# Low weight parts of a float32 hybrid decoder: a negated copy and an adding DMA in place of a subtraction

## The chip, the cores and the metric

One core of a Trainium2 chip runs the kernel. The metric is the device time of one execution in microseconds (us). The core has a matrix engine (TensorE, PE in the rows; its weight loads stand as PEld), VectorE (DVE), ScalarE (ACT), GpSimd (POOL), a queue engine that here only issues transfers (SyncE, SP), and 16 DMA engines that all queues share. Each engine works through its own instructions in a fixed order and waits on semaphores for the others.

## The reference, cut to what matters

Two layers, on 512 tokens of 1024 features, everything in float32. Each layer has one input projection with 78 column tiles of 128, three token mixers (SSD, S5 and latent attention, MLA), and an output projection:

```
for l in range(DEPTH):                       # DEPTH = 2
    h = rms_norm(x, pre_norm[l])
    proj = h @ w_in[l]
    z_a, xbc, dt_raw, u_b, z_b, c_q, c_kv, k_rope, z_c, gate_logits = split_columns(proj)
    y_a = ssd_branch(z_a, xbc, dt_raw, ...) @ w_a[l]
    y_b = s5_branch(u_b, z_b, ..., w_glu[l], b_glu[l]) @ w_b[l]
    y_c = mla_branch(c_q, c_kv, k_rope, z_c, ...) @ w_c[l]
    merged = gates[0] * y_a + gates[1] * y_b + gates[2] * y_c
    x = x + rms_norm(merged @ w_o[l], post_norm[l])
```

## The kernel before, in words

A product of two float32 matrices is made out of three products of rounded numbers. Each operand is split into a high part, rounded to the format `F32R` that TensorE multiplies in one pass, and a low part, the float32 operand minus its high part; the kernel adds high times high, high times low and low times high in PSUM. Weights come from DRAM in blocks of 128 partitions by up to 1024 columns, 512 KiB, and each is used once, for 512 tokens.

`weight` (L85) does this for one block. SyncE loads it into a buffer `wf` (L95, or eight pieces at L93 for one operand of S5), ScalarE writes the rounded copy `wh` (the call at L96, whose instruction carries the helper's line L59), and VectorE writes `wl = wf - wh` (the call at L98, instruction line L71). In the MLA stage every third block and in the SSD stage every second has its subtraction on GpSimd instead (L74; `lo_pool` and the counter `nw` choose). `wf`, `wh` and `wl` have two buffers each, so `wf` of one block is free for the load of the block after the next as soon as the subtraction has read it. `dense` (L101) then runs, per block of 1024 columns, 16 matmuls that read `wh` (L109, L110) and after them 8 that read `wl` (L112), all 128x128 by 512 columns. `mm3` (L52) is the other user: it goes through high-high, high-low and low-high for each 128 rows, so it needs `wl` almost at once (L54 to L56); the first two tiles of each layer (`proj2`), the key and value tiles of MLA and the S5 blocks take that way.

A layer runs in this order: norm and the first projection tiles; MLA, with the preparation of the S5 matrices woven in (mostly multiplications on GpSimd); a scan over 63 steps that lies on VectorE, beside the `w_c` products; SSD; eight S5 blocks, each with two blocks of S5 matrices (`kpad` in pieces, `odr`) that go through `weight` from a pool of their own; then the `w_glu`, gate and `w_b` products, and the output projection. Six of the eight output blocks `w_o` are loaded between the `w_b` products (L1043, L1044): they take a `wf` buffer out of the same two, but are split by `split` (L76) into buffers of their own. The order of the instructions on each engine comes from a scheduler that simulates the program when it is built; it is no part of the source.

Of the kernel before, what the change touches and what calls it, by code (L numbers as in the profile page):

```python
# [17 lines left out]
L = 2  # L18
# [5 lines left out]
# first tile of each part of the input projection, in the host's order  # L24
# [10 lines left out]
class Trunk:  # L35
# [49 lines left out]
    def weight(self, src, n, pool=None):  # L85
        """hi and lo parts of a block of n columns per partition, streamed from DRAM"""
        pool = pool or self.wp
        wf = pool.tile([P, 1024], F32, name="wf", tag="wf", bufs=2)
        wh = pool.tile([P, 1024], F32R, name="wh", tag="wh", bufs=2)
        wl = pool.tile([P, 1024], F32R, name="wl", tag="wl", bufs=2)  # L90
        if isinstance(src, list):
            for rows, x in src:
                self.nc.sync.dma_start(wf[rows, :n].rearrange("p (g k) -> p g k", k=x.shape[-1]), x)  # L93
        else:
            self.nc.sync.dma_start(wf[:, :n], src)  # L95
        self.act_(wh[:, :n], wf[:, :n])  # L96
        self.nw += 1
        (self.gt if self.lo_pool and self.nw % self.lo_pool == 0 else self.tt)(wl[:, :n], wf[:, :n], wh[:, :n].bitcast(F32), ALU.subtract)  # L98
        return wh, wl

    def dense(self, src, rhs, m=P, n=None, main=True):  # L101
        """[m, T] bank of src^T rhs; rhs: (hi, lo) per 128 rows"""
        k = len(rhs)
        wh, wl = self.weight(src, k * m)
        ps = self.bank(main)
        mm = self.nc.tensor.matmul
        o = lambda i: slice(i * m, i * m + m)
        for i, (bh, bl) in enumerate(rhs):
            mm(ps[:m], wh[:, o(i)], bh, start=i == 0, stop=False)  # L109
            mm(ps[:m], wh[:, o(i)], bl, start=False, stop=False)  # L110
        for i, (bh, bl) in enumerate(rhs):
            mm(ps[:m], wl[:, o(i)], bh, start=False, stop=i == k - 1)  # L112
        return ps

    def proj2(self, l, tiles):
        """two tiles of the projection, first for the first half of the tokens"""
# [57 lines left out]
    def sincos_small(self, ang, n):  # L174
# [21 lines left out]
        # sin = 2 s c, cos = 1 - 2 s^2  # L196
# [8 lines left out]
    def rsqrt_mean(self, ss, n, scale, eps=EPS):  # L205
        """(scale * ss + eps) ** -0.5 on n columns"""
# [6 lines left out]
    def rsqrt_rows(self, sq, scale):  # L213
        """sq [128, T]: sums over partitions -> (scale * sum + eps) ** -0.5 along T, on every partition"""
# [13 lines left out]
    def s5_prep(self, l, pp):  # L228
# [27 lines left out]
        # f = (abar - 1) / lambda  # L256
# [18 lines left out]
        # coefficients of the scan over blocks: groups 0..31 on the lower half, 32..63 on the upper  # L275
# [25 lines left out]
        def block(b):  # L301
            """inputs in blocks of 8 steps: (step, channel of the group) on partitions; what depends on B and C alone"""
# [49 lines left out]
        def back(b, s, uf, bb, v1, w1):  # L352
# [19 lines left out]
            if s % 2:  # L372
# [3 lines left out]
                # kernel of the steps within a block  # L376
# [32 lines left out]
    def norm_in(self, tt, xt, G):  # L409
        """RMS norm of a tile of tokens (two halves of its features), transposed and split into self.hh, self.hl"""  # L410
# [15 lines left out]
    def silu2(self, l, tile_, keep=True):  # L426
        """2 silu of a tile of the projection"""
# [24 lines left out]
    def merge(self, l, i, w, acts, m, rrow=None):  # L452
        """merged += 2 sigmoid(gate_i) * (w^T acts) (* rrow along T), a tile of it; its gates run ahead"""
# [137 lines left out]
    def attend_qk(self, mp, q, k, h):  # L591
        """rows of exp(q k^T * SCALE - max), causal; their sums in self.rs"""
# [19 lines left out]
    def attend_v(self, mp, scs, v):  # L612
        """probabilities times v, transposed, as the sum of two parts of [64, T]"""
        nc = self.nc
        # key block kb holds queries kb * 128 ...
# [25 lines left out]
    def ssd_dt(self, l, sp):  # L641
        """dt, its cumulative decays and what depends on tokens and heads alone"""
# [55 lines left out]
    def ssd(self, l):  # L698
        nc, tc, a = self.nc, self.tc, self.a
        with tc.tile_pool(name=f"ssd{l}", bufs=1, reuse_waits="tile") as sp:  # L700
# [12 lines left out]
            def conv(t):  # L713
                """silu of the causal convolution of a tile of channels"""
# [16 lines left out]
            def core(g, xs, zs, bt, ct):  # L731
# [4 lines left out]
                # C B^T per chunk, keys on partitions, masked  # L736
# [7 lines left out]
                # token-major x dt, its decayed form, and B  # L744
# [26 lines left out]
                # states at the chunks' starts  # L771
# [50 lines left out]
            def head(g, hh, cbm):  # L822
                """decayed C B^T of a head, keys on partitions, and its decays along T"""
# [46 lines left out]
    def s5_scan(self, l, sp):  # L870
        """states at the starts of the blocks"""
# [14 lines left out]
    def s5_block(self, l, sp, b):  # L886
        """outputs of 8 groups, and their gelu"""
# [66 lines left out]
    def layer_in(self, l, xs):  # L954
        """xs(t): the two halves of x of a tile of 128 tokens, in SBUF"""
# [7 lines left out]
    def layer(self, l):  # L963
        nc, tc, a = self.nc, self.tc, self.a
        self.first2 = self.proj2(l, (CQ, CQ + 1))
        # rope key and dt
# [17 lines left out]
    def mix(self, l):  # L984
        nc, tc, a = self.nc, self.tc, self.a
        with ExitStack() as st:
# [6 lines left out]
            # the softmax's sums, along T  # L993
# [73 lines left out]
    def wout(self, l, mg, wo, G):  # L1067
        nc = self.nc

        def out_tile(t):  # L1070
# [18 lines left out]
            # the rows are twice the reference's: 0.5 (s / 4 + eps) ** -0.5 = (s + 4 eps) ** -0.5  # L1089
# [52 lines left out]
def _tiles(w):  # L1142
    """[L, K, M] -> [L, M / 128, 128 (row), K / 128, 128 (column)]"""
    l, k, m = w.shape
    w = w.reshape(l, k // P, P, m // P, P).transpose(0, 3, 2, 1, 4)
    return np.ascontiguousarray(w).reshape(l, m // P, P, k)


def layouts(i):
# [31 lines left out]
    # constants  # L1181
# [32 lines left out]
```

## Time and profile before

| | us |
|---|---|
| median of 2 runs | 2004.49 (2004.17 to 2004.82) |
| span of the profiled execution | 2005.7 |
| PE busy | 1890.3 |
| DVE busy | 1451.9 |
| ACT busy | 942.0 |
| POOL busy | 649.9 |

The span goes from the first to the last instruction of one profiled execution. Busy time of matmuls counts each from its start to its modelled end, though the next one starts earlier, so a PE that is nearly always busy can still have room. In the rows, an arrow points from what an instruction reads to what it writes (`wl<-wf,wh`); a bracket gives the idle time before an instruction and what ended it.

### The profile page before, as it was taken

Reading aid. Unit: us, or ns where it says so; the run is one execution under the profiler, and the core shown is the slowest. Engines: PE = TensorE matmul, PEld = TensorE weight load, DVE = VectorE, ACT = ScalarE, POOL = GpSimd, SP = SyncE. Lnnn points to the kernel's source line nnn. Section 1 sums busy time; section 2 is a strip of 40 time slices with the busy share of each in tenths; the row PEclk is TensorE's granted clock in tenths of the full one; section 3 lists DMA queues with packets and bytes.
Section 4 is the critical chain, followed back from the end, with each engine's and each line's share of the span. In section 5 each row is a group of like instructions: output and inputs, shape, how many; then the busy total and the mean of one; then the engine's idle time right before and its main releaser. Section 6 shows DMA issues by size and latency. Waiting matters only on the chain.

```text
span 2005.7 us, 27806 instructions
## 1 busy us (share of the span) xinstructions
PE 1890.3 (94%) x9688; PEld 1524.2 (76%) x9688; DVE 1451.9 (72%) x2845; ACT 942.0 (47%) x1743; POOL 649.9 (32%) x743
## 2 busy tenths in 40 slices
PE   7897999899999989999997999998999999999998
PEld 6685777687877868887875777776878887788786
DVE  7866667699999857744478666677999996776433
ACT  4364566522555445533333655564235563554331
POOL 1855466301333201201118556662013331012010
PEclk9898999899999999999998999998999999999999
DMA  5232234232321266344232333342332224662531
GB/s 166 88 115 83 91 118 128 83 108 74 127 74 64 75 184 181 93 152 157 88 91 83 108 104 111 91 139 82 96 123 77 74 74 111 181 171 84 168 126 42
DMA packets 132605, 219.96 MB, mean 110 GB/s; under 512 B 36208, under 2 KB 75760, under 8 KB 131952
## 3 DMA queue, kind: packets, MB, share of 16 engines
q1 hardware_dynamic: 132464, 218.19, 35.4%
q8 instruction: 76, 1.25, 0.3%
q14 instruction: 65, 0.53, 0.1%
HBM read 182.08 MB, written 31.33 MB: 106 GB/s over the span
## 4 chain that ended last, share of the span: by engine, by line
PE 59%; DVE 25%; DMA 7%; POOL 3%; ACT 3%; issue 2%; SPq 1%; DVEq 0%; POOLq 0%; ACTq 0%
PE mm L109 14%; PE mm L110 13%; PE mm L112 13%; DVE wl L71 4%; DVE keep L62 3%; PE mm L54 2%; PE mm L55 2%; PE mm L56 2%; DMA wf<-in_w_in 2%; DVE ms L882 2%; DVE sc_t L879 2%; PE pk L378 2%; DVE ms L881 1%; PE aux L55 1%; PE aux L54 1%
## 5 line engine op out<-in xcount | busy, mean ns | idle before, releaser
L109 PE MATMUL mm<-hh,wh 128*128 128x512 f32 (+1 forms) x1232 | 501.2, 407 | 16.4 <-DVE ql L71 8.8
L110 PE MATMUL mm<-hl,wh 128*128 128x512 f32 (+1 forms) x1232 | 493.6, 401 | 0.0
L59 ACT ACTIVATE wh<-wf 128x1024 fp32r<-128x1024 f32 (+1 forms) x294 | 291.2, 994 | 423.7 <-PE mm L110 240.8
L71 DVE TENSOR_TENSOR wl<-wf,wh 128x1024 fp32r<-128x1024 f32 (+1 forms) x243 | 297.5, 1229 | 183.8 <-ACT wh L59 149.6
L112 PE MATMUL mm<-hh,wl 128*128 128x512 f32 (+1 forms) x1232 | 315.1, 393 | 2.4 <-DVE wl L71 2.4
L109 PEld LDWEIGHTS mm<-hh,wh 128*128 128x128 f32 (+1 forms) x1232 | 237.2, 193 | 78.6 <-ACT wh L59 10.0
L110 PEld LDWEIGHTS mm<-hl,wh 128*128 128x128 f32 (+1 forms) x1232 | 236.8, 192 | 50.2 <-issue 1.9
L112 PEld LDWEIGHTS mm<-hh,wl 128*128 128x128 f32 (+1 forms) x1232 | 227.5, 187 | 52.0 <-DVE wl L71 3.2
L74 POOL TENSOR_TENSOR mg<-mg,tmp 128x512 f32<-128x512 f32 x32 | 77.7, 2429 | 464.4 <-DVE tmp L71 242.7
L74 POOL TENSOR_TENSOR wl<-wf,wh 128x1024 fp32r<-128x1024 f32 (+1 forms) x51 | 109.5, 2147 | 292.2 <-PE mm L112 186.7
L109 PE MATMUL mm<-ah,wh 128*128 128x512 f32 x512 | 204.1, 401 | 0.1
L110 PE MATMUL mm<-al,wh 128*128 128x512 f32 x512 | 201.2, 394 | 0.0
L112 PE MATMUL mm<-ah,wl 128*128 128x512 f32 x512 | 130.8, 396 | 0.0
L109 PEld LDWEIGHTS mm<-ah,wh 128*128 128x128 f32 x512 | 96.2, 188 | 25.5 <-issue 1.8
L110 PEld LDWEIGHTS mm<-al,wh 128*128 128x128 f32 x512 | 96.2, 188 | 22.1 <-issue 0.5
L112 PEld LDWEIGHTS mm<-ah,wl 128*128 128x128 f32 x512 | 95.7, 188 | 22.6
L602 DVE CUSTOM_DVE_ANT_0 sc<-aux,cmask 128x128 f32<-128x128 f32 (+3 forms) x128 | 60.3, 486 | 50.8 <-PE aux L56 49.1
L59 ACT ACTIVATE sc<-sc,nm 128x128 f32<-128x128 f32 (+3 forms) x128 | 70.3, 553 | 30.3 <-DVE nm L66 30.2
L74 POOL TENSOR_TENSOR pv<-pq,ar 128x288 f32<-128x288 f32 x64 | 56.4, 903 | 85.3 <-PE pk L378 68.3
L71 DVE TENSOR_TENSOR pl<-aux,ph 128x512 fp32r<-128x512 f32 (+1 forms) x96 | 54.8, 594 | 26.2 <-ACT ph L59 25.7
L59 ACT ACTIVATE tmp<-mm 128x512 f32<-128x512 f32 x76 | 44.9, 594 | 60.6 <-PE mm L56 34.1
L62 DVE SCALAR_TENSOR_TENSOR keep<-mm,cw,keep 128x511 f32<-128x511 f32 (+2 forms) x96 | 71.1, 741 | 2.1 <-ACT keep L59 1.5
(344 smaller groups left out, 4079.9 us busy)
## 6 DMA issues: line engine op xcount, KB each, us to landing
wf<-in_w_in SPq DMA_DIRECT2D x156, 512.0 KB
odr<-pv SPq DMA_DIRECT2D x64, 128.0 KB
wf<-in_w_c SPq DMA_DIRECT2D x16, 512.0 KB
wf<-in_w_a SPq DMA_DIRECT2D x16, 512.0 KB
wf<-kpad SPq DMA_DIRECT2D x128, 64.0 KB
wf<-odr SPq DMA_DIRECT2D x16, 512.0 KB
wf<-in_w_glu SPq DMA_DIRECT2D x16, 512.0 KB
wf<-in_w_b SPq DMA_DIRECT2D x16, 512.0 KB
```

Of the source, the lines that this page charges most:

```text
L54: mm(out, ah, bh, start=start, stop=False)
L55: mm(out, ah, bl, start=False, stop=False)
L56: mm(out, al, bh, start=False, stop=stop)
L59: self.nc.scalar.activation(out, in_, func, **kw)
L62: self.nc.vector.scalar_tensor_tensor(out, in0, s, in1, op0, op1)
L71: self.nc.vector.tensor_tensor(out, a, b, op)
L74: self.nc.gpsimd.tensor_tensor(out, a, b, op)
L109: mm(ps[:m], wh[:, o(i)], bh, start=i == 0, stop=False)
L110: mm(ps[:m], wh[:, o(i)], bl, start=False, stop=False)
L112: mm(ps[:m], wl[:, o(i)], bh, start=False, stop=i == k - 1)
L378: nc.tensor.matmul(pk.rearrange("p g k -> p (g k)"), bbp[b % 2][:, q:q + 4].rearrange("p g h -> p (g h)"), v1[:, :, 0:8].rearrange("p g k ...
L602: nc.vector.tensor_tensor_reduce(out=sc, in0=ps[:, :n], in1=self.cmask[:, 512 - n:512], op0=ALU.add, op1=ALU.max, scale=1.0, scalar=-3.0e3 ...
```

## The change

`weight` no longer subtracts. ScalarE makes a second pass over the loaded block and writes `wl = round(-wf)`, which is minus the high part. GpSimd then issues a DMA that adds the float32 block `wf` onto `wl` in SBUF. The sum is `wf - wh` again. `lo_pool` and `nw` are not read any more. `split`, with its subtraction on VectorE, stays for everything that is not a weight of `weight`, the `w_o` blocks among it. The rest of the diff takes comments and docstrings out of the source and changes no instruction.

```
         self.act_(wh[:, :n], wf[:, :n])
-        self.nw += 1
-        (self.gt if self.lo_pool and self.nw % self.lo_pool == 0 else self.tt)(wl[:, :n], wf[:, :n], wh[:, :n].bitcast(F32), ALU.subtract)
+        self.act_(wl[:, :n], wf[:, :n], scale=-1.0)
+        self.nc.gpsimd.dma_start(wl[:, :n].bitcast(F32), wf[:, :n], accum_op=ALU.add)
         return wh, wl
```

## Rows read from the trace of the kernel before

**Rows 1.** Stages of layer 1: busy per engine (instructions), clock, DMA share, GB/s.

```profile
core 0: us, PE busy (x) PEld busy (x) DVE busy (x) ACT busy (x) POOL busy (x), PEclk, DMA share, GB/s
60.00:390.00 330.00, 291.95 (x1459) 234.37 (x1457) 226.22 (x439) 179.08 (x433) 201.65 (x288) 0.92 0.34 100
390.00:500.00 110.00, 108.25 (x459) 85.32 (x459) 100.95 (x340) 30.39 (x41) 7.59 (x4) 0.98 0.28 99
500.00:695.00 195.00, 189.64 (x1036) 152.60 (x1036) 181.08 (x288) 105.78 (x175) 62.34 (x42) 1.00 0.25 86
695.00:835.00 140.00, 133.86 (x890) 110.09 (x889) 92.36 (x107) 69.78 (x98) 15.55 (x8) 0.99 0.58 156
835.00:895.00 60.00, 60.00 (x260) 48.44 (x259) 33.09 (x38) 28.68 (x37) 10.36 (x1) 1.00 0.31 108
895.00:960.00 65.00, 64.91 (x280) 52.06 (x279) 27.70 (x26) 21.11 (x24) 11.26 (x6) 1.00 0.54 180
```

**Rows 2.** The page's chain that ended last: share of the span by engine.

```profile
PE 59%; DVE 25%; DMA 7%; POOL 3%; ACT 3%; issue 2%; SPq 1%; DVEq 0%; POOLq 0%; ACTq 0%
```

**Rows 3.** Groups by shape: busy us, mean ns of one | idle before, by releaser.

```profile
L71 DVE TENSOR_TENSOR wl<-wf,wh 128x1024 fp32r<-128x1024 f32 x217 | 276.6, 1280 | 165.9 <-ACT wh L59 141.6 <-PE mm L112 9.6 <-ACT tmp L59 5.8
L59 ACT ACTIVATE wh<-wf 128x1024 fp32r<-128x1024 f32 x252 | 265.0, 1056 | 358.3 <-PE mm L110 197.6 <-DMA wf<-in_w_in 44.0 <-DMA wf<-kpad 27.0
L74 POOL TENSOR_TENSOR wl<-wf,wh 128x1024 fp32r<-128x1024 f32 x35 | 88.1, 2516 | 272.3 <-PE mm L112 175.2 <-ACT wh L59 64.7 <-PE aux L750 16.7
```

**Rows 4.** Order of time in the glu products: start, duration, engine, instruction.

```profile
859.66 1.06 ACT L59 ACTIVATE wh<-wf 128x1024 fp32r<-128x1024 f32 x1 [2.98 <-PE mm L110]
861.59 1.23 DVE L71 TENSOR_TENSOR wl<-wf,wh 128x1024 fp32r<-128x1024 f32 x1 [3.77 <-ACT wh L59]
861.59 0.69 ACT L59 ACTIVATE tmp<-mm,bglu 128x512 f32<-128x512 f32 x1 [0.87 <-PE mm L112]
865.26 1.06 ACT L59 ACTIVATE wh<-wf 128x1024 fp32r<-128x1024 f32 x1 [2.98 <-PE mm L110]
```

**Rows 5.** The same in the w_b products: a load's issue and its consumer.

```profile
936.98 0.33 SPq L1044 DMA_DIRECT2D wf<-in_w_o  x1
940.34 1.06 ACT L59 ACTIVATE woh<-wf 128x1024 fp32r<-128x1024 f32 x1 [0.93 <-DMA wf<-in_w_o]
```

**Rows 6.** Longest pieces of the chain, w_b products: start, us.

```profile
932.77 1.81 PE mm L112 x8
943.82 1.81 PE mm L112 x8
```

**Rows 7.** DMA of 870 to 880 us in 40 slices; issues of 695 to 835 us.

```profile
GB/s 295 393 426 377 197 66 0 0 0 0 0 0 0 0 0 0 0 66 0 0 180 213 360 262 426 262 180 147 66 0 0 0 0 0 0 0 0 0 0 0
...
wf<-in_w_in SPq DMA_DIRECT2D x11, 512.0 KB
wf<-kpad SPq DMA_DIRECT2D x64, 64.0 KB
wf<-odr SPq DMA_DIRECT2D x8, 512.0 KB
wf<-in_w_a SPq DMA_DIRECT2D x6, 512.0 KB
```

**Rows 8.** DVE's groups in the SSD stage, 500 to 695 us.

```profile
L71 DVE TENSOR_TENSOR wl<-wf,wh 128x1024 fp32r<-128x1024 f32 x15 | 18.3, 1220 | 0.3 <-ACT wh L59 0.3
L71 DVE TENSOR_TENSOR xdl<-tmp,xdh 128x512 fp32r<-128x512 f32 x8 | 13.8, 1741 | 0.8 <-ACT xdh L59 0.7
```

**Rows 9.** The chain of 390 to 500 us, by line.

```profile
by line: DVE sc_t L879 17.3%; DVE wl L71 15.3%; DVE ms L882 14.8%; DVE ms L881 11.4%; DVE sc_t L880 10.1%; PE mm L109 5.7%; PE mm L110 4.9%; DVE keep L62 4.7%; DVE mg L62 3.9%; issue 3.1%; PE mm L112 2.1%; PE aux L1009 1.5%; DVE d_p L62 1.0
```

**Rows 10.** GpSimd beside VectorE at the end of the S5 blocks, order of time.

```profile
835.25 10.36 POOL L74 TENSOR_TENSOR mg<-mg,tmp 128x512 f32<-128x512 f32 x1 [8.59 <-DVE tmp L71]
836.23 6.77 DVE L62 SCALAR_TENSOR_TENSOR al<-gl,ah 128x512 fp32r<-128x512 f32 x6
```

**Rows 11.** PE's waits in MLA: waited for, total us, times, longest.

```profile
PE mm L55 <- POOL wl L74: 5.8, 1, 5.8
```

## The prediction

> **What bounds the kernel now.** I read the stages first, then the chain of waits, then the groups of the weight path, then the order of time inside two stages. In the stages [rows 1] the reader is to see that PE is the bound nearly everywhere outside MLA: it is busy for all 60 us of the glu products, 64.9 of 65 of the w_b products, 108 of 110 beside the scan, 190 of 195 in SSD. Only MLA leaves it idle for 38 of 330 us, at a clock of 0.92. VectorE is close behind in two stages, 101 of 110 us in the scan and 181 of 195 in SSD, and the DMA engines stand out in one, 0.58 of the S5 blocks' 140 us. The chain says the same: PE 59%, DVE 25% [rows 2]. In the scan's stage 15.3% of the chain, 17 us, is the subtraction of weights itself [rows 9].
>
> The weight path hides behind PE today. ScalarE's rounding waits mostly for PE to give back a buffer (`PE mm L110`, 198 of the 358 us of its idle time) and hardly for a load [rows 3]. In the glu products the rounding starts every 5.60 us, each time when PE has finished with the `wh` of two blocks earlier, and VectorE's subtraction starts when the `wl` of two blocks earlier is free [rows 4]. The `wl` is ready 1.23 us later and PE wants it when the next rounding starts at 870.86 at the earliest (one more period after 865.26), so it lies there for some 8 us. This slack is what the change spends.
>
> **What the change removes and adds.** A layer sends 147 blocks through `weight` (78 + 1 tiles of the projection, 12 of `w_uq`, 8 of `w_ukv`, 32 of the four square products, 16 of S5), so there are 294. Of the 252 large ones, VectorE loses 217 subtractions, 277 us, and GpSimd 35, 88 us [rows 3]. ScalarE gains as many passes as it rounds, 252 x 1.06 = 265 us for the large ones [rows 3], which lifts it from 942 to over 1207 of 2006 us, still no bound. And GpSimd's queue gets 294 transfers, the large ones 132 MB.
>
> The second pass of ScalarE waits for `wl` to come free, that is for PE's L112, where VectorE waited before. Behind it on ScalarE stands, in the glu products, the tanh that waits for the same matmuls [rows 4]; it starts 1.06 us later and nothing is late by it. On GpSimd the transfer waits for that pass; behind it stand the multiplications of the S5 preparation in MLA and the additions into `mg`. They have slack, but now every late block holds that queue too.
>
> **The price of one add.** No GpSimd transfer is in this trace, so each part is bounded.
> - Issue on GpSimd: SyncE's issue takes 0.33 us [rows 5]; a GpSimd pass over the same block takes 2.52 [rows 3]. It writes descriptors and reads no block, so I take 1.0, nearer the first.
> - Start and receipt: a load issued at 936.98 has its consumer start at 940.34, which waited for it [rows 5]: 3.36 us. At its best the queue moves some 400 GB/s [rows 7], 1.3 us for a block of 0.524 MB. 3.36 less 1.3 and less 0.33 is 1.7.
> - Data: an add reads two blocks and writes one. It could cost as much as a copy, 1.3 us, or three copies at the 333 GB/s that the w_b stage shows in its busy time (180 over 0.54, [rows 1]), 4.7. I take two copies, 2.6, since two reads share the way in.
>
> A rule of the skill bears on the last: the Trainium skill, "Collectives: The Full Stack", section "The bandwidth ceiling: the fold count and why AG ≠ RS ≠ AR", says that a reduction in the DMA runs at half the rate of a copy because of its second source read, not because of the addition. By it the data part would be twice a copy, too; no run here shows it yet.
>
> So 1.0 + 1.7 + 2.6 = 5.3 us from the end of ScalarE's pass to a usable `wl`; 3.4 at the low ends, 8.9 at the high ones. PE can wait for `wl` that long in the glu products (8 us). But `wf` is now held until the add is over, and that is the loop to look at: load 3.36, two passes of 1.06, add 5.3, and some 0.3 for the hand-overs, an estimate: 11.1 us for one buffer, against 3.36 + 1.06 + 1.23 + 0.2 = 5.85 before.
>
> **Stage by stage, for one layer.**
> - Products of one block after another (scan, glu: some 28 blocks): two buffers, so 11.1 / 2 = 5.55 us per block against PE's 5.60 [rows 4]. Nothing, but without margin: each further us costs 0.5 x 28 = 14 us.
> - w_b with w_o between: three users take turns at two buffers, two weights at 11.1 and one w_o at 5.85. One round takes 28.05 / 2 = 14.0 us; before it is 11.05 (943.82 less 932.77, [rows 6]), set by PE. Six rounds: +18 us.
> - S5 blocks: the DMA engines are busy 0.58 x 140 = 81 us [rows 1]. The loads listed are 11 + 8 (64 pieces of kpad) + 8 + 6 = 33 blocks [rows 7]; 33 adds of 2.6 us are 86. 167 us of transfers into 140: +27.
> - The layer's first block: `proj2` wants `wl` at once, so it is late by 1.06 + 5.3 - 1.23: +5.
> - MLA: 16 blocks go through `mm3`. PE once waited 5.8 us there for a subtraction of GpSimd's [rows 11]; with one in five late by 3 us I take +8, an estimate between nothing and 16 times 3.
> - Scan and SSD: VectorE is freed of 17 us of chain [rows 9], of 18 in SSD, and of some 9 us by which its eight `xdl` (1.74 us, where half a `wl` takes 0.64) seem drawn out beside GpSimd's subtractions [rows 3, 8]. That is 44 us, but PE has only 7 us of visible idle time there [rows 1]. Between 7 and 44 I take 15, nearer PE's: -15.
>
> Sum: 18 + 27 + 5 + 8 - 15 = +43 us, twice +86. The profiled span is 2005.7, so 2092; the median of the runs is 1.2 lower than the span, so I say 2090.
>
> **Rivals.**
> 1. Hidden. At the low ends (0.33 + 1.7 + 1.3 = 3.4) the loop takes 9.1 us, w_b costs 12.0 against 11.05, +6, the S5 blocks need 81 + 43 = 124 of 140 us, nothing, the start +3. With the -15 that is -6 a layer: 1994. For it speaks the slack in [rows 4]; against it the second read.
> 2. Faster: VectorE's chain in scan and SSD opens up. If all 44 us reached the end and the add was as cheap as in 1, 6 + 3 - 44 = -35 a layer: 1936. It takes 30 of the 44 for 2%. For it, VectorE is 92% busy in both stages and leads the chain in one [rows 1, 9]; against it, PE's 98 and 97% there.
> 3. A slow add, three copies: 1.0 + 1.7 + 4.7 = 7.4, loop 13.2. Then the 28 blocks cost 1.0 each, +28, w_b 16.1 a round, +30, the S5 blocks 81 + 155 = 236 into 140, +96, start +7, MLA +15, less 15: +161 a layer, 2328. The load list [rows 7] speaks for it: the S5 blocks break first.
> 4. GpSimd is held off. One addition of GpSimd's takes 10.36 us while VectorE runs a row of operations with two operands in SBUF [rows 10]. If the issue of an add is drawn out like the subtractions were, to 2.5 us, the loop grows by 1.5: 28 x 0.7 = +20, w_b +9, MLA +5, start +1.5 on top of my sum: 79 a layer, 2163. The Trainium skill, "SBUF — State Buffer", section "Who interferes with whom", has VectorE's two-port modes shut GpSimd out for the whole instruction, descriptors of its transfers among it; two-operand operations it counts only against GpSimd's reads. By it few adds would be held here, and this rival would be rarer than the row makes it look.
>
> **How the numbers follow.** Forecast 0.38, hidden 0.22, faster 0.13, slow add 0.15, held off 0.12. Faster by over 2% is 0.13, within 2% 0.22, slower by over 2% the other three, 0.65; 2% is about what a measurement can tell from no change. The time is the forecast's, 2090, whose own range is 2050 to 2160. The whole range runs from 1985, which leaves out the faster case, to 2330, the end of the slow add: about 0.82 of the chance.
>
> **What would show it.** GpSimd's issue near 1.0 us, and near 5.3 us from it to the matmul or load that waited; a copy's data time or three tells rivals 1 and 3. The DMA share should go from 0.25 to about 0.6 in SSD, and to near 1 in the S5 blocks. In the w_b products SyncE's loads should wait for the adds, and L112 of every second block stand 14 us apart. Rounding should wait for loads where it waited for PE. ScalarE should be over 1207 us. VectorE at 1175 or below with PE's gaps unchanged in SSD would say that the -15 was too much. The forecast falls if the loop stays below PE's 11.2 us, or if the scheduler, which orders by its own simulation, places the adds so late on GpSimd that MLA pays more than the S5 blocks.

## The result, and the profile after

The changed kernel takes 2303.04 us (2298.31 to 2307.77), 1.148 times the kernel before (95% interval 1.142 to 1.155). The forecast was 2090, with a range of its own from 2050 to 2160 and a whole range from 1985 to 2330: slower, as predicted, but by 299 us where 86 were worked out. The profiled execution of after spans 2296.5 us, 290.8 more than that of before.

The page of after, the chain by engine and line, and three groups of the weight path (busy us, mean ns of one | idle before, by releaser):

```profile
DMA 38%; PE 33%; ACT 8%; issue 8%; DVE 7%; POOL 4%; SPq 1%; POOLq 0%; ACTq 0%; DVEq 0%
DMA wl<-wf 12%; DMA sf<-sdr 8%; PE mm L109 7%; PE mm L112 7%; DMA wf<-in_w_in 7%; PE mm L110 7%; ACT wh L59 2%; ACT wl L59 2%; PE mm L55 2%; PE mm L54 2%; PE mm L56 2%; DMA bc<-in_s_bc 1%; DMA wf<-in_w_b 1%; POOL pv L74 1%; DMA wf<-kpad 1%
...
L98 POOL DMA_DIRECT2D wl<-wf x294 | 257.0, 875 | 1016.5 <-ACT wl L59 769.2
L59 ACT ACTIVATE wh<-wf 128x1024 fp32r<-128x1024 f32 (+1 forms) x294 | 291.8, 993 | 544.4 <-DMA wf<-in_w_in 259.6
...
L112 PE MATMUL mm<-hh,wl 128*128 128x512 f32 (+1 forms) x1232 | 327.3, 404 | 24.7 <-DMA wl<-wf 24.4
```

In the chain the DMA engines went from 7% to 38% and PE from 59% to 33% [rows 2]. Rounding, which waited for PE [rows 3], now waits for loads. PE waits for two things, the rounded blocks, whose loads come late, and the low parts (us in total, times, longest):

```profile
PE mm L109 <- ACT wh L59: 90.2, 35, 11.0
PE mm L112 <- DMA wl<-wf: 48.7, 37, 5.2
PE pM L55 <- DMA wl<-wf: 39.5, 18, 4.8
```

With `L55` and `L56` of the other products, PE waited 113.3 us for adds; before, it waited 10.2 us for subtractions. The loads come late because they wait for their buffers, as SyncE's queue shows:

```profile
SPq L95 <- DMA wl<-wf: 1044.0, 193, 15.8
```

PE's idle time in the span grew by 207 us (2296.5 less 1974.3 against 2005.7 less 1890.3). The other 84 us of the longer span are busy time, for the same 9688 matmuls. The granted clock fell meanwhile from 0.970 to 0.940 of full speed; as it is either 1.2 or 2.4 GHz, it was at the lower level for 12% of the span instead of 6%.

The stages of layer 1 in after, to be read beside [rows 1] (MLA, scan, SSD, S5 blocks, glu, `w_b`; the edges are moved by the time that each stage grew):

```profile
core 0: us, PE busy (x) PEld busy (x) DVE busy (x) ACT busy (x) POOL busy (x), PEclk, DMA share, GB/s
60.00:423.00 363.00, 314.64 (x1518) 246.17 (x1517) 183.02 (x408) 213.98 (x485) 197.16 (x315) 0.93 0.59 142
423.00:529.00 106.00, 99.33 (x419) 76.86 (x418) 76.70 (x320) 39.06 (x48) 12.92 (x15) 0.97 0.72 189
529.00:724.00 195.00, 190.84 (x1051) 155.95 (x1050) 155.32 (x274) 132.79 (x204) 56.13 (x59) 1.00 0.60 147
724.00:937.00 213.00, 159.51 (x914) 126.64 (x913) 56.75 (x76) 102.83 (x133) 41.46 (x43) 0.86 0.79 193
937.00:1005.00 68.00, 60.37 (x239) 45.99 (x237) 19.44 (x25) 35.05 (x44) 10.41 (x11) 0.95 0.63 152
1005.00:1102.00 97.00, 78.58 (x306) 59.84 (x307) 11.78 (x14) 34.30 (x38) 18.25 (x19) 0.95 0.75 196
```

With edges at the same instructions in every kernel, the stages can be compared, though the scheduler orders each kernel anew and some matmuls then lie on the other side of an edge. In the table, "MLA" goes from the start of the layer to the last score row (`sc`), "scan" from there to the first `cbm` of SSD, "SSD" to the last `ssq`, "S5" from the first issue of `sf` to the last `ys`, "glu" to the last tanh of `w_glu`, "w_b" to the first product with `woh`. The output products and the 4 to 8 us ahead of S5 are left out. Each entry is layer 1 / layer 2, from the start times in the traces.

| kernel | MLA | scan | SSD | S5 | glu | w_b |
|---|---|---|---|---|---|---|
| before | 367.8/347.4 | 144.8/148.0 | 180.2/169.3 | 130.6/131.2 | 64.4/64.5 | 74.9/74.5 |
| after | 401.2/380.6 | 140.9/144.0 | 179.6/178.2 | 202.4/202.1 | 71.9/71.4 | 107.2/104.2 |
| e1 no add | 346.9/340.2 | 128.3/133.6 | 180.1/178.1 | 130.0/129.3 | 65.1/65.1 | 79.1/78.7 |
| e6 buffer held, adds | 404.6/385.0 | 147.8/146.4 | 194.8/191.5 | 191.4/194.6 | 67.1/69.5 | 98.7/97.6 |
| e8 adds, not held | 398.8/381.6 | 144.9/147.5 | 194.0/176.7 | 193.2/193.4 | 67.5/67.5 | 83.1/84.5 |
| e9 held, few bytes | 381.8/365.3 | 142.7/145.8 | 188.7/182.6 | 142.7/137.0 | 64.3/64.5 | 77.9/78.1 |
| e7 three buffers | 396.3/366.3 | 140.9/135.2 | 175.1/174.1 | 205.5/204.0 | 65.1/64.9 | 97.1/97.0 |
| e12 `sf` spread | 400.7/378.9 | 142.4/142.0 | 182.4/180.6 | 164.7/163.9 | 71.6/71.9 | 108.4/108.3 |
| e15 `sf`, `msd` spread | 377.6/374.3 | 140.9/137.0 | 182.4/181.5 | 165.1/163.3 | 72.0/72.6 | 107.1/105.8 |
| e13 before, spread | 365.2/342.6 | 145.0/143.5 | 176.8/170.8 | 123.0/122.8 | 64.6/64.5 | 74.4/75.0 |

The loss per layer is S5 +72 and +71, MLA +33 and +33, `w_b` +32 and +30, glu +7 and +7, less some 4 in the scan; SSD is level in layer 1 and +9 in layer 2. The +9 can't be put down to the adds: e1, which has none, shows it too, and the stage holds 981 matmuls for 951 before, the scan ahead of it 553 for 600. S5 alone makes half of it, and S5 is where the forecast missed most (+27).

### The profile page after: what moved, and what is told of

It reads as the page before. It is cut to its first block, busy times and chain, and to the rows that moved or that the text cites. A ratio compares the mean times of both kernels' runs of the same rounds, so it can differ in the third digit from the quotient of the medians.

```text
span 2296.5 us, 28479 instructions
## 1 busy us (share of the span) xinstructions
PE 1974.3 (86%) x9688; PEld 1562.7 (68%) x9688; DVE 1132.5 (49%) x2602; ACT 1187.6 (52%) x2037; POOL 716.9 (31%) x986
## 3 DMA queue, kind: packets, MB, share of 16 engines
q0 software_dynamic: 42336, 143.02, 32.7%
## 4 chain that ended last, share of the span: by engine, by line
DMA 38%; PE 33%; ACT 8%; issue 8%; DVE 7%; POOL 4%; SPq 1%; POOLq 0%; ACTq 0%; DVEq 0%
DMA wl<-wf 12%; DMA sf<-sdr 8%; PE mm L109 7%; PE mm L112 7%; DMA wf<-in_w_in 7%; PE mm L110 7%; ACT wh L59 2%; ACT wl L59 2%; PE mm L55 2%; PE mm L54 2%; PE mm L56 2%; DMA bc<-in_s_bc 1%; DMA wf<-in_w_b 1%; POOL pv L74 1%; DMA wf<-kpad 1%
## 5 line engine op out<-in xcount | busy, mean ns | idle before, releaser
L109 PE MATMUL mm<-hh,wh 128*128 128x512 f32 (+1 forms) x1232 | 517.2, 420 | 72.3 <-ACT wh L59 70.7
L98 POOL DMA_DIRECT2D wl<-wf x294 | 257.0, 875 | 1016.5 <-ACT wl L59 769.2
L110 PE MATMUL mm<-hl,wh 128*128 128x512 f32 (+1 forms) x1232 | 509.7, 414 | 0.0
L112 PE MATMUL mm<-hh,wl 128*128 128x512 f32 (+1 forms) x1232 | 327.3, 404 | 24.7 <-DMA wl<-wf 24.4
L109 PEld LDWEIGHTS mm<-hh,wh 128*128 128x128 f32 (+1 forms) x1232 | 246.9, 200 | 139.9 <-ACT wh L59 81.0
L59 ACT ACTIVATE wl<-wf 128x1024 fp32r<-128x1024 f32 (+1 forms) x294 | 290.4, 988 | 12.3 <-PE mm L55 5.9
L112 PEld LDWEIGHTS mm<-hh,wl 128*128 128x128 f32 (+1 forms) x1232 | 229.4, 191 | 84.9 <-DMA wl<-wf 34.3
L110 PEld LDWEIGHTS mm<-hl,wh 128*128 128x128 f32 (+1 forms) x1232 | 246.6, 200 | 53.6 <-issue 1.7
L112 PE MATMUL mm<-ah,wl 128*128 128x512 f32 x512 | 134.4, 405 | 13.7 <-DMA wl<-wf 13.4
L112 PEld LDWEIGHTS mm<-ah,wl 128*128 128x128 f32 x512 | 96.8, 192 | 40.4 <-DMA wl<-wf 18.9
L74 POOL TENSOR_TENSOR mg<-mg,tmp 128x512 f32<-128x512 f32 x32 | 50.9, 1589 | 156.4 <-DVE tmp L62 101.5
L62 DVE SCALAR_TENSOR_TENSOR keep<-mm,cw,keep 128x511 f32<-128x511 f32 (+2 forms) x96 | 71.4, 744 | 54.5 <-ACT keep L59 53.3
L71 DVE TENSOR_TENSOR wol<-wf,woh 128x1024 fp32r<-128x1024 f32 x16 | 19.4, 1220 | 134.4 <-ACT woh L59 134.4
L62 DVE SCALAR_TENSOR_TENSOR keep<-tmp,keep 128x512 f32<-128x512 f32 x48 | 35.2, 734 | 95.9 <-ACT tmp L59 95.8
```

What stands on the lines that cost most here:

```text
L59: self.nc.scalar.activation(out, in_, func, **kw)
L62: self.nc.vector.scalar_tensor_tensor(out, in0, s, in1, op0, op1)
L71: self.nc.vector.tensor_tensor(out, a, b, op)
L74: self.nc.gpsimd.tensor_tensor(out, a, b, op)
L98: self.nc.gpsimd.dma_start(wl[:, :n].bitcast(F32), wf[:, :n], accum_op=ALU.add)
```

## The experiments

**First, the parts of the change.** Two runs keep ScalarE's second pass and take the add away, or make a copy of it (the first leaves the low parts out, the second puts the block itself in their place).

```
-        self.nc.gpsimd.dma_start(wl[:, :n].bitcast(F32), wf[:, :n], accum_op=ALU.add)      # e1
+        self.nc.gpsimd.dma_start(wl[:, :n].bitcast(F32), wf[:, :n])                        # e2, in its place
```

> The changed kernel without the adding DMA: wl is minus the rounded block, so the low part of every weight of the weight path is left out and only its cost in ScalarE passes stays. Theory (the block's buffer, held until the add is over, makes the loops): with no add the buffer is free after ScalarE's second pass, each loop is 3.4 + 1.06 + 1.06 + 0.2 = 5.7 us, and the time goes back to 1985 to 2010. Rival A (ScalarE's second pass, which waits for wl where VectorE waited before, costs by itself): 2040 or more. Rival B (VectorE's freed 277 us were worth something and the add ate it): below 1965.

> The changed kernel with a plain copy in place of the add, same queue, same block, same waits: wl becomes the block itself, so the low parts are wrong. Theory (held buffer): an add took 2.7 us of the DMA engines and 5.3 us to land; a copy should take 1.3 to 1.6 and land in 4.0, loops shrink by 1.3 us and more where transfers crowd; S5 stage of a layer from 202 to about 165, w_b from 107 to 90, in all 2150 to 2200. Rival (the DMA engines' throughput alone): S5 needs 81 + 45 of 132 us, so S5 and w_b go back to what they were before, in all 2060 to 2100. Rival (the second read of an add is free): 2290 to 2310.

e1 took 1966.66 us, 0.980 of before (0.978 to 0.982). That is under the theory's 1985 to 2010: relieving VectorE and GpSimd of the subtractions is worth 40 us where nothing has to be added. ScalarE's second pass costs nothing that shows in the total, though `w_b` is 4 us longer in each layer. e2 took 2154.36 us, 1.074 (1.070 to 1.078), about half of the way to the changed kernel and inside the theory's 2150 to 2200; its S5 stage, 175.4 and 178.8 us, stays above the 165 that were expected. Queue 0 of both and the issues (count, KB each, median us to landing), of after and then of e2:

```profile
q0 software_dynamic: 42336, 143.02, 32.7%
wl<-wf POOLq DMA_DIRECT2D x252, 512.0 KB, 5.3
```

```profile
q0 software_dynamic: 39616, 143.02, 17.2%
wl<-wf POOLq DMA_DIRECT2D x252, 512.0 KB, 3.2
```

For the same 143.02 MB the adds occupy the 16 engines for 0.327 x 2296.5 = 751 us each, the copies for 0.172 x 2155.0 = 371: twice.

**Then, the source of the add.** In e3 the add reads the weights from DRAM a second time instead of `wf` (all but S5's operands), in e4 S5's operands too, so that no add holds a load buffer.

```
-        self.nc.gpsimd.dma_start(wl[:, :n].bitcast(F32), wf[:, :n], accum_op=ALU.add)
+        self.nc.gpsimd.dma_start(wl[:, :n], src.bitcast(F32R), accum_op=ALU.add)
```

> The add takes its block from DRAM again instead of from wf, for all weights but those of the S5 blocks: wf is free after ScalarE's second pass, the DMA engines do as much as in the changed kernel. Theory (held buffer): w_b stage of a layer from 107 to 80 us, MLA from 287 to 265, scan and glu 5 less, S5 as before at 195 to 205; in all 2190 to 2220. Rival (throughput of the DMA engines): no change, 2290 to 2310. Rival for MLA alone (wl comes too late for PE, not wf): MLA stays at 285, w_b shrinks, in all 2235 to 2255.

> As the run before, and the S5 blocks' adds take their block from DRAM too (the kpad operand in 8 pieces, so 8 issues of GpSimd, some 0.6 us each, in place of one). Theory (each S5 operand has one buffer per block, so load, two passes and add follow one another): S5 stage from 202 to 165 to 175, the 163 us that the DMA engines are busy there and a little; in all 2120 to 2150. Rival (the DMA engines are the bound in S5): S5 stays at 195 to 210, in all as the run before, 2190 to 2220.

Both went the other way: 2386.63 us, 1.188 (1.183 to 1.193), and 2503.26 us, 1.247 (1.243 to 1.251). In e3 the adds of 512 KB land after 7.2 to 10.4 us (medians by source) instead of 5.3. In e4 the add onto `kpad`'s low part is eight issues of 1.99 us each, and the S5 stage takes 289 and 279 us. These runs change the hold and the source at once (e4 the issues, too) and can't part them; they only say that freeing the buffer in this way is no cure.

**Where in the kernel.** e5 is the kernel before with the changed path for S5's two operands alone, 32 of the 294 blocks; e10 is the changed kernel with the old subtraction for just these.

```
+        if pool is not self.wp:                                  # e5, in before
+            self.act_(wl[:, :n], wf[:, :n], scale=-1.0)
+            self.nc.gpsimd.dma_start(wl[:, :n].bitcast(F32), wf[:, :n], accum_op=ALU.add)
+            return wh, wl
```

> The kernel before, with ScalarE's second pass and the adding DMA for the two operands of the S5 blocks alone, 32 of the 294 blocks. Theory (each of these operands has one buffer per S5 block, so load, two passes and add follow one another, some 24 us a block): the S5 stage of a layer goes from 131 to 180 to 200 us, in all 2100 to 2145. Rival A (it is the adds of the other 18 blocks of the stage that slow these loads, whose packets are small, on the shared DMA engines): S5 at most 145, in all at most 2035. Rival B (DMA engines' throughput: 81 + 16 x 2.7 = 124 of 131 us): no change, 2000 to 2015.

> The changed kernel, but the two operands of each S5 block (kpad, odr: 32 of 294 blocks) go back to VectorE's subtraction. Theory (S5's own operands wait in a loop of one buffer each): S5 goes from 202 to 150 to 165 us a layer, since 17 adds remain beside its loads; 2303 less 2 x 37 to 2 x 52: 2200 to 2230. Rival (S5 is bound by the sum of its transfers, 163 us of 202): 16 adds of 2.7 us less a layer, 43 us of transfers, the same size, but then DMA share stays near 0.8 in the stage; by the loop it falls to 0.7 or below, with PE as what it waits for. Rival (the stages do not add up): 2250 to 2300.

e5: 2089.26 us, 1.042 (1.039 to 1.045), a little under the theory's 2100 to 2145; its S5 stage takes 174.9 and 179.4 us. Part of that is moved work: the stage holds 916 and 914 matmuls for 840 before, and glu is 15 and 14 us shorter, so that S5 and glu together are 30 and 34 us longer. Another 20 us lie in MLA of layer 2, where e5 issues no add; why is not known. e10: 2246.41 us, 1.120 (1.116 to 1.124), S5 169.1 and 173.4, so 57 us less than after where 74 to 104 were expected. The DMA share of e10's S5 stage is 0.73, between what the two theories said. A ninth of the blocks costs over a quarter of the loss in e5 and a fifth in e10.

**The hold against the traffic.** In three variants of the kernel before, `wl` is made in time by the old subtraction and an adding DMA goes onto scratch in DRAM: e6 from `wf` (held and full traffic), e8 from `wh` (traffic, `wf` not held), e9 from 16 partitions of `wf` (held, an eighth of the bytes).

```
+        self.nc.gpsimd.dma_start(self.scr[self.nw % 4][:, :n], wf[:, :n], accum_op=ALU.add)                  # e6
+        self.nc.gpsimd.dma_start(self.scr[self.nw % 4][:, :n], wh[:, :n].bitcast(F32), accum_op=ALU.add)      # e8
+        self.nc.gpsimd.dma_start(self.scr[self.nw % 4][0:16, :n], wf[0:16, :n], accum_op=ALU.add)             # e9
```

> The kernel before, VectorE and GpSimd subtracting as they did, and beside it GpSimd issues for every block an adding DMA of wf onto a scratch block in DRAM that nobody reads: wf is held as long as in the changed kernel and the DMA engines do as much, but wl is ready in time and ScalarE has no second pass. Theory (the held buffer): close to the changed kernel, 2240 to 2310. Rival (PE waits for a wl that comes late): 2020 to 2080, since no PE instruction waits for an add. Between them, 2100 to 2220, both have a part.

> The kernel before, with an adding DMA for each of the 294 blocks as in the hold run, but its source is the rounded block wh and not the loaded block wf (it goes onto scratch in DRAM; wl is made in time by the old subtraction). So the DMA engines carry the same adds at the same moments, and wf is free after the old subtraction. Theory (the loop of a load buffer: load + passes + add, with the load itself drawn out by the adds; the loop counts only while the add is in it): S5's block needs 10.6 + 2.1 = 12.7 us for a load and its passes, under PE's 16.3, w_b's loop about 8 of 11; what is left is S5's pure throughput, at most 163 us into 131 = +32 a layer: 2010 to 2080. Rival (the DMA engines' time alone, whoever is held): as the hold run, 2250 to 2300. Between the two, 2100 to 2240: the drawn out loads by themselves cost a share, which the S5 and w_b stages would show.

> The kernel before, with an adding DMA from each loaded block wf onto scratch in DRAM, of 16 of its 128 partitions only: an eighth of the bytes, and wf is still held until the DMA has landed. Theory (loop): the hold is issue 0.9 + start and receipt 1.7 + data 0.3 = 2.9 us in place of 5.3, beside loads that are hardly drawn out: w_b's loop about 3.4 + 1.1 + 2.9 + 0.5 = 7.9 for each of two, 10.9 a round with the w_o block against 11.1, nothing; S5's block 8 + 2.9 + 1.1 = 12 under 16.3, nothing; 2005 to 2050. Rival (any DMA that holds wf stops SyncE's queue of loads in order, whatever it weighs): 2120 to 2250.

e6 took 2298.22 us, 1.146 (1.142 to 1.149), as long as the changed kernel, though no matmul waits for an add there: a loss of this size needs no late low part. That the times are equal is partly chance. e6 relieves neither VectorE nor GpSimd, against after its SSD is 15 and 13 us longer and its S5 11 and 8 shorter, and its adds, onto DRAM, are heavier: 838 us of each DMA engine (0.365 x 2295.6) and 6.3 us to landing, where after has 751 and 5.3. e8 took 2251.68, 1.121 (1.118 to 1.124), and here my theory of the held buffer fell: it said 2010 to 2080. Its adds are as heavy (856 us) and they hold `wh`, for which rounding waited 60.4 us, so it overstates the traffic somewhat. e9 took 2083.55, 1.037 (1.033 to 1.042), above the theory's 2005 to 2050. By stage they agree on a division: in `w_b` the hold costs (98.7 with it, 83.1 without), in S5 the bytes do (193.2 with no hold, 142.7 with a hold and few bytes).

**A third load buffer.** e7 is the changed kernel with three buffers of `wf` (`tmp` gives up two of seven).

```
-        wf = pool.tile([P, 1024], F32, name="wf", tag="wf", bufs=2)
+        wf = pool.tile([P, 1024], F32, name="wf", tag="wf", bufs=3 if pool is self.wp else 2)
```

> The changed kernel with three wf buffers instead of two for all blocks but S5's, paid for with five instead of seven of the 2 KiB tmp tiles. Theory (held buffer): the w_b round, three users of two buffers, 15.0 us, becomes one of three buffers, under PE's 11.1, so the w_b stage goes from 107 to about 80 us; MLA loses the 80 us in which SyncE waits for adds there and goes from 287 to about 270; S5 unchanged; in all 2200 to 2240. Rival (late wl in MLA): MLA stays at 285, in all 2240 to 2260. Rival (neither; the missing tmp tiles cost more): over 2300.

2244.86 us, 1.118 (1.115 to 1.120), just above the theory's 2200 to 2240: 58 us back, in `w_b` (10 and 7 us), glu (7 and 7), SSD (4 and 4), MLA (5 and 14) and layer 2's scan (9), and nothing in S5, whose operands come from a pool of their own. In `w_b` the theory had expected 27 us: the stage takes 97 us and not 80. With three buffers its `w_b` loads are still 15.4 us apart in places (issued at 1029.23 and 1044.66), and SyncE's queue still waits 77 us there for adds (75 in after).

**What the bytes do in S5.** The chain of after in the S5 blocks (start, us), with its three longest pieces:

```profile
by line: DMA sf<-sdr 40.9%; DMA wl<-wf 15.8%; DMA wf<-in_w_in 8.0%; DMA wf<-kpad 7.9%; issue 5.6%; ACT wl L59 3.3%; DVE sl L71 2.3%; PE mm L109 2.2%; PE mm L110 2.2%; DMA wf<-odr 2.0%; ACT wh L59 2.0%; DMA wf<-in_w_a 1.7%; ACT sh L59 1.4%; 
...
800.59 18.33 DMA sf<-sdr
...
847.90 17.97 DMA sf<-sdr
...
895.11 17.94 DMA sf<-sdr
```

`sf` is no weight: it is the load of the scan's states (L894), 256 KB. At the start of S5 in the trace of before, with no adds about, the same piece of the chain is 7.66 us long, and later in that stage the load is hidden. SyncE's issues in one block, of before and of after (start, us from the first to the last, line):

```profile
739.38 0.51 SPq L894 DMA_DIRECT2D sf<-sdr  x1
739.93 2.85 SPq L93 DMA_DIRECT2D wf<-kpad  x6
742.88 0.37 SPq L95 DMA_DIRECT2D wf<-odr  x1
```

```profile
847.90 0.51 SPq L894 DMA_DIRECT2D sf<-sdr  x1
852.59 13.59 SPq L93 DMA_DIRECT2D wf<-kpad  x8
866.29 0.36 SPq L95 DMA_DIRECT2D wf<-odr  x1
```

The pieces of `kpad` behind `sf` take 13.59 us to issue where six took 2.85, and the loads after them are issued only then. Half of it is the eighth piece, whose issue waits until `sf` has landed. SyncE's waits of this kind in the whole run of after, for 16 loads of `sf` (us in total, times, longest):

```profile
SPq L93 <- DMA sf<-sdr: 82.5, 16, 8.8
```

In before they come to 64.6 us, which PE's work covers; with `sf` spread, in e12 below, to 1.0. The DMA engines at the end of that stretch, 862 to 866 us of after in 40 slices of 0.1 us (busy share in tenths, GB/s):

```profile
DMA  0022002200220022002200220012101111111111
GB/s 0 20 61 41 0 20 61 41 0 20 61 41 0 20 61 41 0 20 61 41 0 20 61 41 0 20 41 61 41 20 41 41 61 41 41 36 41 41 41 46
```

Nearly all engines are idle, and on about two of them something alternates. The packets recorded there are 2 KB ones of `sf`, 98 ns each, and 4 KB ones of the add, 327 ns each, in turn. So `sf` lies on about two of the 16 engines, and each of its packets waits for one of the add's. Its source has 2 as outermost dimension (real and imaginary part): one load, `p r g c -> r p g c`. The Trainium skill, "DMA: Bandwidth & Descriptors", section "Rules for kernel authors", states this: an outermost dimension below 16 keeps the whole transfer on at most as many engines; the trace agrees, with its two. The sum fits as well: with no adds 7.66 us, and the four adds of a block occupy each engine for 4 x 751 / 273 = 11.0 us (273 full blocks' worth, 252 and 42 smaller ones as halves), together 18.7 against the measured 17.5 to 18.3 (one load of the stage took 11.3). To test it, the load is issued as two, of 64 partitions each:

```
-        sh, sl = load(self.sdr[b // 4, :, :, 8 * (b % 4):8 * (b % 4) + 8].rearrange("p r g c -> r p g c"), "s")
+        sh, sl = load([(slice(64 * r, 64 * r + 64), self.sdr[b // 4, :, r, 8 * (b % 4):8 * (b % 4) + 8]) for r in range(2)], "s")
```

> The changed kernel; the only edit is that the load of the S5 states (sf, 256 KB) is issued as two loads of 64 partitions each instead of one load whose outermost dimension is 2. In the trace of the changed kernel that load seems to lie on two of the 16 DMA engines: between 862 and 866 us the DMA share alternates between 0 and 2 tenths, and its pieces in the chain are 17.3 to 18.3 us long, about 64 packets of 2 KB on one engine at 90 ns (5.8 us) and 4 adds x 8 packets of 327 ns (10.5 us) between them, and 2 us of start and receipt. Theory (the adds' packets stand between the packets of this narrow load, and the load holds SyncE's queue): S5 falls from 202 us to what its transfers need, 163 to 175 a layer: 2225 to 2250. Rival (the held buffers or the sum of the transfers make the stage): no change, 2285 to 2310.

> The run with the DMA traffic alone (2251.7, S5 193 us a layer), with the load of the S5 states spread as in the run above. Theory: S5 falls to 150 to 170, since no buffer is held either: 2252 less 2 x 23 to 2 x 43, 2165 to 2205. Rival (sum of transfers, 170 us, at the share of 0.88 that the stage already has): 2240 to 2260.

e12, the changed kernel: 2227.58 us, 1.110 (1.106 to 1.113), 75 us below after, inside the range, and of the stages only S5 moved by more than 5 us, from 202 to 164.7 and 163.9. e14, the traffic alone: 2172.39 us, 1.083 (1.080 to 1.087), inside too, S5 from 193 to 158.4 and 159.1. S5's stage in before, after, e8 and e12, in this order (columns as above):

```profile
697.70:828.30 130.60, 124.46 (x840) 102.49 (x840) 87.13 (x102) 63.76 (x90) 15.55 (x8) 0.99 0.62 168
```

```profile
728.30:930.70 202.40, 148.91 (x859) 117.99 (x858) 51.37 (x69) 96.10 (x127) 39.16 (x42) 0.86 0.81 196
```

```profile
741.30:934.60 193.30, 142.39 (x836) 116.17 (x836) 85.52 (x101) 64.39 (x92) 42.64 (x43) 0.82 0.88 200
```

```profile
732.10:896.80 164.70, 139.37 (x858) 112.91 (x857) 51.08 (x69) 96.40 (x126) 39.02 (x42) 0.91 0.99 239
```

In after the 16 engines were busy for 0.81 x 202.4 = 164 us, and with `sf` spread 0.99 x 164.7 = 163. The work did not change; the idle time of the engines went from 38 us to 2.

**The same in MLA, and without adds.** The store of the scan's inputs (`msd`, 256 KB, eight a layer) has the same form. e15 spreads it too; e13 spreads both in the kernel before.

```
-                nc.sync.dma_start(msd[b // 4, :, :, 8 * (b % 4):8 * (b % 4) + 8].rearrange("p r g c -> r p g c"), mo)
+                for r in range(2):
+                    nc.sync.dma_start(msd[b // 4, :, r, 8 * (b % 4):8 * (b % 4) + 8], mo[64 * r:64 * r + 64])
```

> The changed kernel with both transfers spread, sf and msd (8 stores of 256 KB a layer, in MLA and after it). Theory (the same delay of a narrow transfer costs part of MLA's +33 us a layer): 5 to 15 us a layer below the run that spreads sf alone: 2195 to 2235. Rival (MLA waits for late low parts and held buffers only): the same as the run that spreads sf alone, within 8 us.

> The kernel before, no adds; the load of the S5 states (sf) and the store of the scan's inputs (msd), both with an outermost dimension of 2, are each issued as two transfers. Theory: without adds they are hidden but for the first sf load of a layer, 7.7 us in the chain before, which becomes about 3.5: 1994 to 2002. Rival (hidden altogether, or the additional issues on SyncE cost as much): 2003 to 2012.

> The changed kernel with both narrow transfers spread and a third load buffer for the weights (7 buffers of tmp become 5 to make room). Theory (three causes side by side: narrow transfers between the adds' packets, load buffers held until the add has landed, the rest from late low parts): the third buffer's gain of 58 us comes on top, since it lies in MLA and w_b and not in S5: 2188 less 45 to 65, 2120 to 2145. Rival (the third buffer had won by hiding the delays of the narrow transfers): 2160 to 2190.

e15: 2187.96 us, 1.089 (1.086 to 1.092), 40 below e12, more than the theory's 2 x 15; MLA 23 us shorter in layer 1 and 5 in layer 2. In layer 1's MLA the granted clock rose with it from 0.94 to 0.98, and 14 of the 23 us are PE's busy time (337.0 to 323.3). e13: 1977.16 us, 0.984 (0.981 to 0.987), 1.6% below the kernel before, clear of noise, and more than expected: S5 falls by 7.6 and 8.4 us, MLA by 2.6 and 4.8. So in layer 2's MLA the spreading gives no more with adds than without. e16, e15 with a third buffer: 2133.75 us, 1.064 (1.060 to 1.067), inside 2120 to 2145. The narrow transfers and the held buffer are separate terms that add up.

**VectorE's gain.** e11 gives every second subtraction beside the scan to GpSimd (`lo_pool = 2` there, in before). e17 uses the changed path beside the scan alone, 28 blocks, in the kernel of e13.

```
+                self.lo_pool = 2              # e11; 0 again behind the w_c products
                 self.s5_scan(l, sp)
...
+        if self.lo_dma:                       # e17; set from s5_scan to the last w_c product
+            self.act_(wl[:, :n], wf[:, :n], scale=-1.0)
+            self.nc.gpsimd.dma_start(wl[:, :n].bitcast(F32), wf[:, :n], accum_op=ALU.add)
+            return wh, wl
```

> The kernel before, but in the stage beside the scan every second subtraction of weights goes to GpSimd, as it already does in SSD: no DMA. The run without the add won 15 us a layer there when VectorE and GpSimd were both free of all subtractions. Theory (VectorE's work leads there, GpSimd is idle): half of that, 1985 to 2000. Rival (GpSimd's subtraction takes 2.5 us or more beside VectorE's, so wl is late for PE): 2003 to 2020. Rival (PE is the bound there anyway): 2000 to 2008.

> The kernel before with both narrow transfers spread, and the changed weight path (minus the rounded block by ScalarE, adding DMA) only for the blocks that are loaded beside the scan (w_c and its gates), where VectorE's chain leads and the DMA engines are free. The changed kernel gained 4 us a layer in that stage, the run without the add 15. Theory (the VectorE gain is real where the add is hidden): 3 to 10 us a layer under the spread kernel alone (1977): 1957 to 1971. Rival (the add's late low parts take back what VectorE gives): 1972 to 1985.

e11: 2029.33 us, 1.011 (1.009 to 1.013): 1.1% slower, and beyond all three expectations; SSD is 7 and 9 us longer, the scan stage not shorter. e17: 1979.50 us, 0.986 (0.984 to 0.988), no gain on e13 and in the rival's range, though not for the rival's reason. The scan stage and SSD of e13, then of e17, layer 1:

```profile
365.20:510.30 145.10, 139.09 (x596) 107.72 (x596) 130.25 (x393) 50.19 (x83) 16.20 (x18) 0.94 0.31 106
510.30:687.10 176.80, 173.80 (x954) 141.66 (x953) 166.34 (x271) 97.90 (x162) 56.80 (x40) 0.98 0.21 71
```

```profile
361.30:497.50 136.20, 131.77 (x554) 101.03 (x555) 113.05 (x375) 57.17 (x91) 24.75 (x30) 0.94 0.57 155
497.50:684.20 186.70, 182.75 (x996) 148.86 (x995) 174.05 (x277) 101.70 (x167) 60.29 (x41) 0.98 0.23 73
```

The scan is 9 us shorter and SSD 10 us longer: 42 matmuls have moved across the edge (596 + 954 and 554 + 996 are both 1550), and PE's busy time over the two is 312.9 and 314.5 us of some 322. PE's idle time over the two is the same, 9.0 and 8.4 us: what VectorE gives, PE's own work takes back in the next stage.

## Why the forecast was right and where it was wrong

Per layer 43 us were forecast and 141 and 146 measured in the stages. Of what is missing S5 has 45 us, MLA 20, `w_b` 12 to 14, glu 7, scan and SSD together 10 to 20. The direction was right, the size was not, and the step that failed most is the S5 term.

- **The price of one add: right.** Issue 0.875 us against 1.0, and from issue to landing a median of 5.3 us against 5.3. The data part is 751 / 273 = 2.75 us against 2.6, and e2 shows the factor of two against a copy. That is also what the rule of the Trainium skill in "Collectives: The Full Stack", section "The bandwidth ceiling: the fold count and why AG ≠ RS ≠ AR", gives for a second source read; this trace agrees. Rival 3, the slow add, thus came near the time (2328) for a wrong reason, by chance: its data part, 4.7 us, did not happen.
- **w_b: the mechanism right as far as it was tested, the size short.** The loop of the held buffer is in the chain of after, two weights and one `w_o` in turn, 29.94 us from one `w_b` load to the next (1041.64 to 1071.58), so 15.0 a round against 14.0 forecast and 11.05 before [rows 6]:

```profile
1047.51 5.40 DMA wl<-wf
...
1052.97 3.51 DMA wf<-in_w_in
...
1058.87 4.59 DMA wl<-wf
...
1063.51 5.71 DMA wf<-in_w_o
```

  I had taken the loads from rows without adds, 3.36 us [rows 5]; `w_o`'s now takes 4.25 and 5.71. Six rounds make 24 us. Of the rest of +32 and +30, 4 us come without any add (e1); what is left was not broken down. For the hold speaks e6 against e8 (98.7 and 83.1); that a third buffer gave back 10 and 7 us and not 27 says that the loop is not the two buffers alone.
- **S5: the term that failed, +72 for +27.** The step was "167 us of transfers into 140". The 167 was right: 164 us of busy time were measured, and with `sf` spread the stage takes 164.7. But the DMA share, which was to go to near 1, was 0.81 and came to 0.99 only with `sf` spread. What failed is that I let the stage be as long as the sum, as if every engine could always be fed. The stage had a transfer on two engines in it, hidden before; between the adds' packets it took 18 us, and SyncE's queue behind it left the other engines idle. That costs 38 us of the 72 (202.4 less 164.7). My list of issues [rows 7] counted blocks and bytes and did not ask how many engines a transfer spreads over. The other 34 are the sum of the transfers, as forecast, but against a stage of 130.6 and not the window of 140.
- **MLA: +33 for +13.** The stage holds two terms of the sum, +8 and the +5 of the layer's first block. That block's products took 9 us more in layer 1 (25.2 for 16.1) and no more in layer 2. I priced late low parts alone, and those too low: PE waited 29.9 and 19.6 us for adds in this stage, 5.8 and 0.0 for subtractions before. 15.7 and 8.7 of it are `L112` matmuls, which I left out; and of `mm3` blocks I counted 16 where the kernel has 8 here, those of `w_ukv`. Besides, the runs show `msd` between the adds (23 and 5 us back in e15, with the clock's part in it) and then the buffer (e16, 4 and 13 more). e9 costs 14 and 18 us there with an eighth of the bytes; how that divides between GpSimd's queue and the held buffers was not settled.
- **Products one after another, glu: nothing was forecast, "without margin", and it is +7.** The third buffer gives it back.
- **Scan and SSD, -15 forecast: -4 in layer 1, +5 in layer 2.** Of the bounds 7 and 44 even the low one was too high. VectorE was freed as said (1132.5 us busy, `xdl` 1277 to 811 ns on average) and the scan became shorter, but the work of PE moved on to SSD (layer 2: 47 matmuls fewer in the scan, 30 more in SSD). e1, with no adds, gains 17 and 6 us in the two stages together, and 21 and 7 in MLA.
- **Rival 4, GpSimd held off: no.** 294 issues took 0.875 us on average. By the rule of the Trainium skill, "SBUF — State Buffer", section "Who interferes with whom", few adds would be held; the trace agrees, with its 0.875 us. Rivals 1 and 2 needed a cheaper add.

Left open: e9's excess over the loop, 34 us above the range's end; the rest of `w_b`; and how MLA's +33 divides between late low parts, held buffers, `msd` and PE's longer busy time.

## What to carry to other kernels

Before bytes are added to a stage, look for transfers that lie on few DMA engines: hidden as long as the stage has slack, they become the stage when wide transfers stand between their packets, and a mean DMA share of 0.6 does not show them. A transfer with a small outermost dimension can be issued as several, which paid 1.6% here, for one load and one store, without any other change. Moving an operation from an engine to a DMA moves its wait to the buffer that the DMA reads, and to whoever needs the result: sum the loop of that buffer with loads as slow as they are beside the new traffic, and count every reader that comes soon.

## What the runs showed of the hardware

- An adding DMA within SBUF occupies the DMA engines twice as long as a copy of the same bytes (751 and 371 us for 143.02 MB), takes 875 ns of GpSimd to issue against 561, and lands after 5.3 us against 3.2 (512 KB).
- A load of 256 KB whose outermost dimension is 2 ran on about two of the 16 engines: 7.66 us with no adds about, 17.5 to 18.3 beside adds, where its 2 KB packets of 98 ns stand in turn with 4 KB packets of the adds of 327 ns.
- An issue of SyncE can wait for the landing of a transfer eight issues earlier: in after its issues of `kpad` waited 82.5 us for `sf`, and eight of 64 KB took 13.59 us where six took 2.85.
- VectorE's `xdl` (128 x 512) took 0.67 to 0.69 us with nothing of GpSimd's beside it, and 2.5 to 2.9 us the four times, all in layer 1 of before, that a subtraction of GpSimd's ran with it.
- The granted clock was lower where PE was idle more: in layer 1's S5 stage of after PE was idle for 54 of 202 us and the clock was 0.86; before, 6 of 131 us and 0.99.
